# Fixed orders in the dense part and the routing, and expert weights in runs of 32 KB into five places

## The chip, the cores and the metric

The kernel runs on one core of one Trainium2 chip, in one launch. The metric is device time in microseconds (us), the median of several executions. Five engines work side by side: TensorE (matrix products; PE in the profile, its weight loads PEld), VectorE (DVE), ScalarE (ACT), GpSimd (POOL) and SyncE (SP), which here issues nearly all transfers between the chip's memory (HBM) and the on-chip memory (SBUF). Matrix products land in PSUM, a small memory of accumulators.

## The reference

Two transformer layers over 256 tokens of width 1024, in float32; all weights are read once.

```python
# first layer
n = rmsnorm(x, norm_mix_pre); proj = n @ w_in        # pool part, q/k/v, memory query, gates
merged = g0 * pool(...) @ w_pool_o + g1 * stick_breaking(q, k, v) @ w_sb_o \
       + g2 * cross(xq, rmsnorm(mem, norm_mem) @ w_mem_kv) @ w_x_o
h = x + rmsnorm(merged @ w_out, norm_mix_post)
n2 = rmsnorm(h, norm_ffn_pre); gu = n2 @ w_ffn_in
h = h + rmsnorm((silu(gu[:, :2816]) * gu[:, 2816:]) @ w_ffn_out, norm_ffn_post)
# second layer
h = rms_norm(x, g_mix); parts = h @ w_in_2           # two attentions, an index, two gates
x = x + (sig(ga) * (o_a @ w_proj_a) + sig(gb) * (o_b @ w_proj_b)) @ w_out_2
# 32 experts, each token goes to the best 2 of the 8 in its best group
for each token's two experts e:
    x += gate * ((silu(xt @ w1[e]) * (xt @ w3[e])) @ w2[e])      # 1024 -> 512 -> 1024
out = rms_norm(x, g_final)
```

The experts' weights are 32 x 3 x 1024 x 512 floats, 201 MB; all other weights are 107 MB.

## The kernel before

**Dense part.** Each float32 product is made of three products of split values: an operand is split into a high part (ScalarE copies it to a shorter format, line 179) and a low part (VectorE, seldom GpSimd, subtracts, line 180), and `mm3` multiplies high by high, high by low and low by high (lines 226 to 228). Weights come in chunks of 1 MB (8 KB in each of 128 partitions) into `ring`, four buffers; a chunk is split into two or more "pieces", whose low parts stand in `lows` or `swing`. A chunk's buffer is free when it has been split, and the next load waits for that on SyncE.

The 256 tokens are two tiles (`tt` 0 and 1). `ts_pair` makes 512 columns of a projection for both tiles, piece by piece; `t_unit` makes a transposed block of 256 columns; `rows_mm` makes an output projection over 1024 columns into four accumulators, at its end with `tt_major=True`: all remaining products of tile 0 first, then those of tile 1. Behind it stand `post_norm_add` (norm of the sums, added to `x`) and `normed_T` (norm of `x`, eight transposes `xtp` on TensorE, split into `xhi` and `xlo`), for tile 0 and then tile 1. This happens twice: at about 223 us (before the first feed-forward products `gu`) and at about 413 us (before the projection `qiT`). At the start the first projection `pps` is written out by hand, operation by operation, with an order for each engine (`do`, `hi_split`, `lo_split`, `products`, `transposes`, `evicted`). The memory's norm, with its transposes, is written after the query product `xq`, before the products `mk` and `mvps` that need it.

The order in which each engine takes its instructions is set by a planner that simulates the program with costs of its own. `tc.issue_after(i)` ties an instruction behind `i` on its engine; `tc.high_priority()` moves a stretch ahead. `behind` ties each TensorE step of the routing to the one before.

**Routing.** The last output projection, the router's logits, the choice of experts (`route`), the numbering of tokens within an expert (`rank`), and the gathering of an expert group's 4 x 32 token slots (`slots`, products `gat` with a 0/1 matrix `pm`, evicted to `xs`). Gate values (`gs`, `den`, `gt`) are worked out with no fixed place among these.

**Experts.** Eight groups of four experts. For a group, W1 and W3 have eight chunks each (`hb`, lines 1292 to 1294), then W2 has four for the low and four for the high half of the columns (`yb`); a chunk holds 128 rows of all four experts, 1 MB. `slot_mm` (line 1277) makes four products per chunk, one for each expert, on 32 columns of the array; the profile records eight matmuls for them. Two chunks make a pair of 2 MB, one transfer of 16 KB per partition (line 1200). Eleven places of 16 KB per partition take the pairs in turn:

```python
    order = [places[n] for n in "sw mg gs b2 c2 d2 tu o r0 r1 lo".split()]
```

They lie where buffers of the dense part lay, so a place's first load waits until these are done: `sw` swing, `mg` mgp, `gs` the gain rows and scratch, `b2 c2 d2` the second attention's buffers, `tu` the gates and `o` the attention outputs, `r0 r1` the two halves of `ring`, `lo` `lows`. The last two chunks of the first group's W3 go elsewhere (two half loads `whalf` and one `wchunk`). In the last group, W2's high half comes in smaller transfers: two of 1 MB and four of 0.5 MB.

After the last group the output is normed and written (lines 1348 to 1359).

Of the kernel before, what the change touches and what calls it, by code (L numbers as in the profile page):

```python
# [18 lines left out]
P = 128  # L19
# [62 lines left out]
def block_kernel(ctx: ExitStack, tc: tile.TileContext, A, out: bass.AP):  # L82
# [151 lines left out]
    def t_block(dst, pc, c0, k, act):  # L234
        for kt in range(k):
            mm3(dst, (pc[0][:, kt, c0:c0 + P], pc[1][:, kt, c0:c0 + P]),
                (act[0][:, kt, :], act[1][:, kt, :]), kt == 0, kt == k - 1)
# [21 lines left out]
    def ts_mm(dst, pcs, act, tt):  # L259
        for k0, per, pc in pcs:  # L260
            for j in range(per):
                mm3(dst, cut(act, k0 + j, tt), (pc[0][:, j, :], pc[1][:, j, :]), k0 + j == 0, k0 + j == KT - 1)
# [11 lines left out]
    def ts_pair(src, c0, n, act, name, hold=1, after=(), free=0, aside=()):  # L274
# [3 lines left out]
        group, npc, made = [], KT // per, 0  # L278
        for c in range(KT // kk):
            w = ts_load(src, c0, n, c)  # L280
            for h in range(2):
# [15 lines left out]
    def rows_mm(accs, pcs, get, nk, tt_major=False):  # L297
        if tt_major:
            r = None
            for tt in range(NT):  # L300
                with ExitStack() as q:
                    if r is not None:
                        q.enter_context(tc.issue_after(r.ins))
                    for h in range(2):
                        for kt, pc in pcs:
                            act, kk = get(kt)
                            r = mm3(accs[tt][h], cut(act, kk, tt), (pc[0][:, h, :], pc[1][:, h, :]), kt == 0,
                                    kt == nk - 1)
            return
# [32 lines left out]
    def normed_T(src, g, tt, hi, lo):  # L342
# [3 lines left out]
        for hf in range(2):  # L346
# [7 lines left out]
            for j in range(4):  # L354
                kt = hf * 4 + j
                nc.tensor.transpose(b[:, j * P:(j + 1) * P], n[:, kt * P:(kt + 1) * P], ident)
# [128 lines left out]
    lo_split(3, "G")  # L485
# [4 lines left out]
    evicted(0, 1, True)  # L490
    for i in (2, 3):
        products(0, i, LH)
# [61 lines left out]
    mt = mg_tiles()  # L554
    for tt in range(NT):
        normed_T(mem[tt], g_mem, tt, *mt)
# [118 lines left out]
    def project(src, accs):  # L675
# [3 lines left out]
        rows_mm(accs, rows_pieces(src, 2) + rows_pieces(src, 4) + rows_pieces(src, 6), get, KT, tt_major=True)  # L679
# [6 lines left out]
    project("w_out", accs)  # L686
# [69 lines left out]
    rows_mm(accs, rows_pieces(wfo, 2 * nf - 6) + rows_pieces(wfo, 2 * nf - 4) + rows_pieces(wfo, 2 * nf - 2),  # L756
# [17 lines left out]
    for tt in range(NT):  # L774
        post_norm_add(accs[tt], g_post, EPS, tt)
        first.append(normed_T(x[:, tt, :], g_pre, tt, *xt))
    cneg = at.tile([P, 384], F32, name="cneg")
# [16 lines left out]
    def rope_heads(c0, scale, name, pool, *how):  # L794
        o = ts_pair(w2in, c0, 512, xt, name, *how)
# [122 lines left out]
    for name, c0, pool in (("b", 1536, atb), ("a", 0, at)):  # L918
        qT = rope_heads(c0, 0.125, "qT" + name, pool)
        kT = rope_heads(c0 + 512, 1.0, "kT" + name, pool)  # L920
        o = ts_pair(w2in, c0 + 1024, 512, xt, "v" + name)
# [181 lines left out]
    pms, gats, xss = {}, {}, {}  # L1103

    def slots(g, tt, hf):
# [5 lines left out]
        if hf == 0:  # L1111
            nc.vector.tensor_tensor(out=pm, in0=rk[:, tt, es, None].to_broadcast([P, 4, CAP]),
                                    in1=cst("iota")[:, None, :].to_broadcast([P, 4, CAP]), op=ALU.is_equal)
# [8 lines left out]
        if hf == 0:  # L1122
            xss[g] = dn.tile([P, KT, P], F32, name="xs", tag="whi", bufs=3)
        ks = slice(hf * 4, hf * 4 + 4)
        nc.vector.tensor_tensor(out=xss[g][:, ks, :], in0=b.rearrange("p (k t) -> p k t", k=4),  # L1125
                                in1=gk[:, ks, None].to_broadcast([P, 4, P]), op=ALU.mult)
        return last

    with tc.high_priority():
# [36 lines left out]


    ew = A["experts"].rearrange("(g c) p n -> g c p n", g=8)
    W1, W3, W2 = 0, KT, 2 * KT

    wst.close()
    places = {}
    for side, names in (("left", "r0 r1 lo mg sw gs tu o"), ("right", "b2 c2 d2")):
        for n in names.split():
            places[n] = ctx.enter_context(tc.tile_pool(name="pair" + n, bufs=1, side=side, reuse_waits="tile"))
    order = [places[n] for n in "sw mg gs b2 c2 d2 tu o r0 r1 lo".split()]
    turn_of = {"i": 0}
    pairs = {}

    def pair_tile():  # L1180
        p = order[turn_of["i"] % len(order)]
        turn_of["i"] += 1
        return p.tile([P, 4096], F32, name="wpair", tag="w")

    def single(g, c, t, e0, ne):
        v = t[:, :ne * 512]
        nc.sync.dma_start(out=v, in_=ew[g, c // 2, :, c % 2 * 2048 + e0 * 512:c % 2 * 2048 + (e0 + ne) * 512])
        return [v[:, e * 512:(e + 1) * 512].rearrange("p (h n) -> p h n", h=1) for e in range(ne)]

    def eload(g, c, part=None):  # L1190

        if g == 0 and c == W3 + KT - 1:
            return single(g, c, xp.tile([P, 2048], F32, name="wchunk", tag="xlo"), 0, 4)
        if g == 0 and c == W3 + KT - 2:
            return [r for e0 in (0, 2) for r in single(g, c, dn.tile([P, 1024], F32, name="whalf", tag="whi", bufs=3),
                                                       e0, 2)]
        if part is None:
            if c % 2 == 0:
                pairs["t"] = pair_tile()
                nc.sync.dma_start(out=pairs["t"], in_=ew[g, c // 2])  # L1200
            t = pairs["t"]
            if c >= W2 + 4:
                v = t.rearrange("p (h f e n) -> p h f e n", h=2, f=2, e=4)
                return [v[:, :, c % 2, e, :] for e in range(4)]
            v = t.rearrange("p (f e n) -> p f e n", f=2, e=4)
            return [v[:, c % 2, e:e + 1, :] for e in range(4)]

        f = c - W2 - 4
        if f == 0:
            pairs["t"] = pair_tile()  # L1210
        t = pairs["t"].rearrange("p (f n) -> p f n", f=4)
        if part == 1 or f % 2 == 0:
            n = 1024 if part == 1 else 2048
            nc.sync.dma_start(out=t.rearrange("p f n -> p (f n)")[:, f * 1024:f * 1024 + n],
                              in_=ew[g, c // 2, :, part * 2048 + f % 2 * 1024:part * 2048 + f % 2 * 1024 + n])
        return [t[:, f, e * 256:(e + 1) * 256].rearrange("p (h n) -> p h n", h=1) for e in range(4)]
# [203 lines left out]
```

## Time and profile before

| | |
|---|---|
| time, median of 3 runs | 1064.04 us (1063.94 to 1064.76) |
| time of the profiled execution | 1063.62 us |
| its span (first to last instruction) | 1061.8 us |
| TensorE busy | 909.4 us (86%) |
| VectorE / ScalarE busy | 451.2 us (42%) / 352.5 us (33%) |
| mean granted TensorE clock | 0.949 |
| read from HBM | 308.20 MB |

The profile is one execution. Each of the three runs is timed without it. A row of the chain of work is a piece of the path that ended last, followed back from the end; a row in brackets such as "[0.90 <-ACT xhi L179]" gives the time the engine stood before it and what ended that. Matmuls overlap, so a row's time can reach into the next.

### The profile page before, as it was taken

How to read it: one execution, taken by the hardware profiler on the slowest of the kernel's cores; microseconds unless marked ns; L12 is line 12 of the kernel's file. 1: busy time of each engine (PE TensorE's matmuls, PEld its weight loads, DVE VectorE, ACT ScalarE, POOL GpSimd, SP SyncE). 2: the span in 40 equal slices, each digit the busy share in tenths (PEclk: the TensorE clock that was granted, in tenths of full speed). 3: DMA queues.
4: the chain of work that ended last, by engine and by line, in shares of the span. 5: the costliest groups of instructions: out<-in, count | busy, mean ns of one | idle time of the engine just before them, and what ended most of it. 6: DMA issues, size and time to landing. Idle time of an engine off the chain costs nothing.

```text
span 1061.8 us, 14621 instructions
## 1 busy us (share of the span) xinstructions
PE 909.4 (86%) x6159; PEld 649.3 (61%) x6159; DVE 451.2 (42%) x765; ACT 352.5 (33%) x550; POOL 48.4 (5%) x42
## 2 busy tenths in 40 slices
PE   8999999999999999999999999767565756666555
PEld 6989899979999996878889973312121211212112
DVE  6656546776545546779765741110101000101102
ACT  6645765455444443444675431000000000000002
POOL 2000022000000000212000000000000000000000
PEclk9999999999999999999999999888998798978988
DMA  9644366556555523744456789999999999999995
GB/s 364 246 150 159 110 251 222 215 225 212 196 196 174 194 97 121 315 159 159 159 206 270 310 326 427 429 426 429 426 429 425 427 428 427 428 427 427 428 428 245
DMA packets 32857, 310.27 MB, mean 292 GB/s; under 512 B 3985, under 2 KB 5137, under 8 KB 8721
## 3 DMA queue, kind: packets, MB, share of 16 engines
q1 hardware_dynamic: 32496, 309.18, 73.1%
q8 instruction: 51, 0.84, 0.3%
q14 instruction: 22, 0.17, 0.0%
q10 hardware_dynamic: 288, 0.08, 0.0%
HBM read 308.20 MB, written 1.05 MB: 291 GB/s over the span
## 4 chain that ended last, share of the span: by engine, by line
PE 59%; DMA 36%; DVE 2%; ACT 1%; issue 1%; POOL 0%; POOLq 0%; SPq 0%; ACTq 0%; DVEq 0%
DMA wpair<-in_experts_dram 36%; PE gu L227 4%; PE gu L228 4%; PE gu L226 4%; PE gate L228 4%; PE gate L227 4%; PE gate L226 4%; PE fo L227 2%; PE fo L226 2%; PE fo L228 2%; PE hb L1277 2%; PE y L228 2%; PE y L226 2%; PE y L227 2%; PE wo L227 1%; PE wo L226 1%
## 5 line engine op out<-in xcount | busy, mean ns | idle before, releaser
L180 DVE TENSOR_TENSOR wlo<-wchunk,whi 128x1024 fp32r<-128x1024 f32 x146 | 181.5, 1250 | 108.1 <-ACT whi L179 106.5
L1277 PE MATMUL hb<-wpair,xs 128*32 128x512 f32 x1008 | 142.6, 695 | 85.9 <-DMA wpair<-in_experts_dram 80.8
L179 ACT ACTIVATE whi<-wchunk 128x1024 fp32r<-128x1024 f32 (+1 forms) x151 | 156.7, 1048 | 164.2 <-PE gu L227 30.2
L1277 PEld LDWEIGHTS hb<-wpair,xs 128*32 128x32 f32 x1008 | 30.2, 119 | 187.1 <-DMA wpair<-in_experts_dram 119.5
L1277 PE MATMUL yb<-wpair,mw 128*32 128x512 f32 (+1 forms) x544 | 74.2, 678 | 32.0 <-DMA wpair<-in_experts_dram 30.5
L1341 DVE TENSOR_TENSOR x<-x,comb 128x512 f32<-128x512 f32 (+1 forms) x34 | 22.3, 656 | 132.7 <-PE comb L1339 132.6
L228 PE MATMUL gate<-xhi,wlo 128*128 128x256 f32 x256 | 73.3, 287 | 0.0
L226 PE MATMUL gate<-xhi,whi 128*128 128x256 f32 x256 | 73.0, 285 | 0.0
L227 PE MATMUL gate<-xlo,whi 128*128 128x256 f32 x256 | 72.7, 284 | 0.0
L1277 PEld LDWEIGHTS yb<-wpair,mw 128*32 128x32 f32 x544 | 16.9, 122 | 82.9 <-DMA wpair<-in_experts_dram 45.5
L1125 DVE TENSOR_TENSOR xs<-gat,gains 128x512 f32<-128x512 f32 x16 | 11.1, 692 | 117.7 <-PE gat L1117 117.7
L180 DVE TENSOR_TENSOR wsw<-wchunk,wsw 128x1024 fp32r<-128x1024 f32 x35 | 42.8, 1224 | 38.3 <-ACT wsw L179 38.1
L226 PE MATMUL gu<-xhi,whi 128*128 128x256 f32 x192 | 54.0, 281 | 0.0
L228 PE MATMUL gu<-xhi,wlo 128*128 128x256 f32 x192 | 54.0, 281 | 0.0
L227 PE MATMUL gu<-xlo,whi 128*128 128x256 f32 x192 | 53.9, 280 | 0.0
L1304 ACT ACTIVATE mw<-hT 128x512 f32<-128x512 f32 x8 | 4.8, 597 | 144.7 <-PE hT L1302 144.7
L179 ACT ACTIVATE wsw<-wchunk 128x1024 fp32r<-128x1024 f32 (+1 forms) x38 | 39.7, 1047 | 33.8 <-PE gu L228 11.0
L228 PEld LDWEIGHTS gate<-xhi,wlo 128*128 128x128 f32 x256 | 48.2, 188 | 2.2 <-issue 2.2
L227 PEld LDWEIGHTS gate<-xlo,whi 128*128 128x128 f32 x256 | 48.2, 188 | 0.8 <-issue 0.5
L226 PEld LDWEIGHTS gate<-xhi,whi 128*128 128x128 f32 x256 | 48.4, 189 | 0.4 <-issue 0.4
L1336 ACT ACTIVATE ysb<-yb 128x512 f32<-128x512 f32 (+1 forms) x17 | 9.7, 572 | 114.9 <-PE yb L1277 114.9
L1296 ACT ACTIVATE ms<-hb 128x512 f32<-128x512 f32 x8 | 4.8, 597 | 128.4 <-PE hb L1277 128.4
(486 smaller groups left out, 1982.2 us busy)
## 6 DMA issues: line engine op xcount, KB each, us to landing
wpair<-in_experts_dram SPq DMA_DIRECT2D x93, 2048.0 KB, 39.1
wchunk<-in_dense_dram SPq DMA_DIRECT2D x92, 1024.0 KB, 4.9
wchunk<-in_dense_dram SPq DMA_DIRECT2D x6, 512.0 KB, 6.1
wpair<-in_experts_dram SPq DMA_DIRECT2D x2, 1024.0 KB, 35.9
wpair<-in_experts_dram SPq DMA_DIRECT2D x4, 512.0 KB, 25.6
memt<-in_mem_dram SPq DMA_DIRECT2D x2, 512.0 KB, 11.9
wchunk<-in_experts_dram SPq DMA_DIRECT2D x1, 1024.0 KB, 10.0
whalf<-in_experts_dram SPq DMA_DIRECT2D x2, 512.0 KB, 8.5
```

What stands on the lines that cost most here:

```text
L179: a = nc.scalar.activation(hi, src, AF.Copy)
L180: return a, (eng or nc.vector).tensor_tensor(out=lo, in0=src, in1=hi.bitcast(F32), op=ALU.subtract)
L226: nc.tensor.matmul(o, lhsT=lh[0], rhs=rh[0], start=start, stop=False)
L227: nc.tensor.matmul(o, lhsT=lh[0], rhs=rh[1], start=False, stop=False)
L228: return nc.tensor.matmul(o, lhsT=lh[1], rhs=rh[0], start=False, stop=stop)
L1125: nc.vector.tensor_tensor(out=xss[g][:, ks, :], in0=b.rearrange("p (k t) -> p k t", k=4), in1=gk[:, ks, None].to_broadcast([P, 4, P]), op= ...
L1277: nc.tensor.matmul(o[ps, :].rearrange("p (h n) -> p h n", h=m), lhsT=lhsT[:, ps], rhs=w[e], start=first, stop=last, skip_group_check=True, ...
L1296: nc.scalar.activation(s, hb[0], AF.Silu)
L1304: nc.scalar.activation(mw[:, 1, :], b, AF.Copy)
L1336: nc.scalar.activation(y[:, cs], yb[:, :n], AF.Copy)
L1341: nc.vector.tensor_tensor(out=xa, in0=xa, in1=cb[:, :n], op=ALU.add)
```

## The change

It has two parts. In the dense part and the routing, orders are tied that were left to the planner:

- the low part of piece 3 in the first projection moves from GpSimd to VectorE, behind tile 0's evictions;
- `xq` is made in two halves, each set behind the transposes of one tile of the memory;
- `rows_mm` with `tt_major` returns `rest`, which issues the last two of tile 1's twelve steps of three products behind the first tile's transposes;
- `ts_pair` gets `in_order`, used by all second-layer projections but `qiT`;
- the routing issues the first two chunks' products `hb` before the last `slots` step; `xs` of the first half is evicted in four pieces; the gate arithmetic stands behind the last `xs`, and `pm` of group 1 too.

The experts' weights are laid out so that four chunks (a quad) are one run of 32 KB per partition, 4 MB in one transfer, into five places of 32 KB, with one of 16 KB (`d`) for two chunks of the first group only. `mgp` and `swing` move ahead of `ring` in memory so that `ms` joins them, `r` is the whole ring, `lu` is `lows` with the gain rows and scratch, `to` the gates and attention outputs, `b` and `d` the second attention's buffers. In the last group W2's high half comes as one transfer of 2 MB and four of 0.5 MB.

```diff
+    mgp = wst.enter_context(tc.tile_pool(name="mgp", bufs=2, side="left"))
+    swing = wst.enter_context(tc.tile_pool(name="swing", bufs=2, side="left"))
     ring = wst.enter_context(tc.tile_pool(name="ring", bufs=4, side="left"))
     lows = wst.enter_context(tc.tile_pool(name="lows", bufs=2, side="left"))
-    mgp = wst.enter_context(tc.tile_pool(name="mgp", bufs=2, side="left"))
-    swing = wst.enter_context(tc.tile_pool(name="swing", bufs=2, side="left"))
...
                     for tt in range(NT):
-                        ts_mm(o[tt][:, :n], group, act, tt)
+                        with ExitStack() as q:
+                            if r is not None and in_order:
+                                q.enter_context(tc.issue_after(r.ins))
+                            r = ts_mm(o[tt][:, :n], group, act, tt)
...
+            todo = [(h, kt, pc) for h in range(2) for kt, pc in pcs]
+            for a in todo:
+                r = one(0, *a)
+            with tc.issue_after(r.ins):
+                for a in todo[:-2]:
+                    one(1, *a)
+
+            def rest(ins):
+                with tc.issue_after(ins.ins):
+                    for a in todo[-2:]:
+                        one(1, *a)
+            return rest
...
     hi_split(3)
-    lo_split(3, "G")
     products(0, 3, HH)
     scaled(1)
     products(0, 2, HL)
     transposes(1)
     evicted(0, 1, True)
+    lo_split(3, "V")
     for i in (2, 3):
         products(0, i, LH)
     products(0, 3, HL)
...
-    b = t_unit(w, xt, "xq")
+    b = t_tile("xq")
+    mt = mg_tiles()
+    r = ()
+    for tt in range(NT):
+        pc = piece(w[:, :, tt * P:(tt + 1) * P], KT, P)
+        normed_T(mem[tt], g_mem, tt, *mt, r)
+        with tc.issue_after(turned_last[tt].ins):
+            r = (t_block(b[:, tt * S:(tt + 1) * S], pc, 0, KT, xt),)
...
     for tt in range(NT):
         post_norm_add(accs[tt], g_post, 4 * EPS, tt)
         first.append(normed_T(x[:, tt, :], g_pre, tt, *xt))
+        if tt == 0:
+            rest(turned_last[0])
...
+    for side, names in (("left", "ms r lu to"), ("right", "b d")):
+        for n in names.split():
+            places[n] = ctx.enter_context(tc.tile_pool(name="place" + n, bufs=1, side=side, reuse_waits="tile"))
+    order = [places[n] for n in "ms b to r lu".split()]
...
+        if part is None:
+            if c % 4 == 0:
+                held["t"] = place_tile()
+                nc.sync.dma_start(out=held["t"], in_=ew[g, c // 4])
...
         route(1)
-        for tt, hf in ((0, 1), (1, 0), (1, 1)):
+        for tt, hf in ((0, 1), (1, 0)):
             behind(lambda: slots(0, tt, hf))
-
-
+        hbs = {0: acc_tile("hb")}
+        for kt in range(2):
+            behind(lambda: slot_mm(hbs[0][0], xss[0][:, kt, :], eload(0, W1 + kt), kt == 0, False))
+        behind(lambda: slots(0, 1, 1))
+
+    gq = ExitStack()
+    gq.enter_context(tc.issue_after(xs_last[0].ins))
```

## Rows read from the trace of the kernel before

**Rows 1.** The page: moved data in 40 slices; the chain's shares.

```profile
GB/s 364 246 150 159 110 251 222 215 225 212 196 196 174 194 97 121 315 159 159 159 206 270 310 326 427 429 426 429 426 429 425 427 428 427 428 427 427 428 428 245
...
PE 59%; DMA 36%; DVE 2%; ACT 1%; issue 1%; POOL 0%; POOLq 0%; SPq 0%; ACTq 0%; DVEq 0%
```

**Rows 2.** Windows, TensorE: us of the window, busy (records), clock, DMA share, GB/s.

```profile
474.00:600.00 126.00, 126.00 (x929) 1.00 0.55 202
```

**Rows 3.** Timeline of SP's issues, 597 to 634 us: start, us, line, transfer.

```profile
597.57 0.33 SPq L1200 DMA_DIRECT2D wpair<-in_experts_dram  x1
...
600.76 0.33 SPq L1200 DMA_DIRECT2D wpair<-in_experts_dram  x1
...
602.74 0.33 SPq L1200 DMA_DIRECT2D wpair<-in_experts_dram  x1
...
613.74 0.33 SPq L1200 DMA_DIRECT2D wpair<-in_experts_dram  x1
...
620.32 0.33 SPq L1200 DMA_DIRECT2D wpair<-in_experts_dram  x1
...
633.16 0.33 SPq L1200 DMA_DIRECT2D wpair<-in_experts_dram  x1
```

**Rows 4.** Windows, transfers: us, clock, DMA share, GB/s.

```profile
610.00:640.00 30.00, 1.00 0.88 338
640.00:1036.00 396.00, 0.88 1.01 427
1038.00:1041.00 3.00, 1.00 1.00 419
1043.00:1046.00 3.00, 0.67 1.02 412
```

**Rows 5.** Chain of work in order of time, 610 to 720 us.

```profile
631.24 13.87 PE hb L1277 x128
...
677.00 39.09 DMA wpair<-in_experts_dram
```

**Rows 6.** Instructions of the tile `wpair`: its transfers from issue to landing.

```profile
DMA to landing us min/median/max: 7.9/39.1/40.8
```

**Rows 7.** Timeline of the start, VectorE, GpSimd and TensorE.

```profile
6.54 0.88 DVE L435 TENSOR_SCALAR ntok<-x,rsr 128x512 f32<-128x512 f32 x2 [0.67 <-POOL rsr L430]
...
13.61 2.98 DVE L435 TENSOR_SCALAR ntok<-x,rsr 128x512 f32<-128x512 f32 x2
...
13.46 2.44 POOL L409 TENSOR_TENSOR wlo<-wchunk,whi 128x1024 fp32r<-128x1024 f32 x1 [0.49 <-ACT whi L406]
...
16.25 1.11 PE L442 MATMUL xtp<-ck,ntok 128*128 128x128 f32 x8 [1.62 <-DVE ntok L435]
```

**Rows 8.** Timeline of TensorE at the memory's norm.

```profile
70.19 0.39 PE L226 MATMUL mvps<-wsw,mgh 128*128 128x256 f32 x1 [1.12 <-ACT mgh L179]
```

**Rows 9.** Timeline of TensorE at the first feed-forward norm.

```profile
224.51 0.50 PE L226 MATMUL gu<-wsw,xhi 128*128 128x512 f32 x1 [0.45 <-ACT xhi L179]
```

**Rows 10.** Timeline of TensorE at the second layer's norm.

```profile
415.23 0.47 PE L226 MATMUL qiT<-wsw,xhi 128*128 128x512 f32 x1 [0.90 <-ACT xhi L179]
...
422.63 1.29 PE L356 MATMUL xtp<-ck,ntok 128*128 128x128 f32 x8 [0.67 <-DVE ntok L349]
```

**Rows 11.** Chain of work at the second layer's norm, 413 to 425 us.

```profile
412.99 0.23 PE fo L227
...
417.52 1.22 DVE wlo L180
...
419.34 1.80 DVE wlo L180 x2
```

**Rows 12.** Timeline of TensorE at the third projection of the second layer.

```profile
472.97 0.50 PE L226 MATMUL qTa<-whi,xhi 128*128 128x512 f32 x1 [0.74 <-DVE vb L924]
```

**Rows 13.** Timeline of TensorE at the end.

```profile
1041.20 4.48 PE L1277 MATMUL yb<-wpair,mw 128*32 128x512 f32 x32 [2.60 <-DMA wpair<-in_experts_dram]
...
1050.16 1.67 PE L1277 MATMUL yb<-wpair,mw 128*32 128x256 f32 x24
```

More of the change, by code (lines that the diff above doesn't have):

```diff
@@ L272, in ts_load, with ts_pair @@
         return t.rearrange("p (k n) -> p k n", k=kk)
-    def ts_pair(src, c0, n, act, name, hold=1, after=(), free=0, aside=()):
+    def ts_pair(src, c0, n, act, name, hold=1, after=(), free=0, aside=(), in_order=False):
         o = acc_tile(name)
@@ L277, in ts_pair @@
         per = kk // 2
-        group, npc, made = [], KT // per, 0
+        group, npc, made, r = [], KT // per, 0, None
         for c in range(KT // kk):
@@ L298, in rows_mm, with one @@
         if tt_major:
[L299 to L309, printed above, removed]
+            def one(tt, h, kt, pc):
+                act, kk = get(kt)
+                return mm3(accs[tt][h], cut(act, kk, tt), (pc[0][:, h, :], pc[1][:, h, :]), kt == 0, kt == nk - 1)
+            todo = [(h, kt, pc) for h in range(2) for kt, pc in pcs]
[9 more added lines that the diff above has]
+            return rest
         for kt, pc in pcs:
@@ L794, in rope_heads @@
     def rope_heads(c0, scale, name, pool, *how):
-        o = ts_pair(w2in, c0, 512, xt, name, *how)
+        o = ts_pair(w2in, c0, 512, xt, name, *how, in_order=not how)
         if how:
@@ new lines, in block_kernel, with place_tile, by_chunk, single @@
+    turn_of = {"i": 0}
+    held = {}
+    def place_tile():
+        p = order[turn_of["i"] % len(order)]
+        turn_of["i"] += 1
+        return p.tile([P, 8192], F32, name="wquad", tag="w")
+    def by_chunk(t, m):
+        v = t.rearrange("p (f e n) -> p f e n", f=m, e=4)
+        return [[v[:, f, e:e + 1, :] for e in range(4)] for f in range(m)]
+    def single(g, c, t, e0, ne):
+        v = t[:, :ne * 512]
+        o0 = c % 4 * 2048 + e0 * 512
+        nc.sync.dma_start(out=v, in_=ew[g, c // 4, :, o0:o0 + ne * 512])
+        return [v[:, e * 512:(e + 1) * 512].rearrange("p (h n) -> p h n", h=1) for e in range(ne)]
@@ new lines, in eload @@
+    def eload(g, c, part=None):
+        if g == 0 and c == W3 + KT - 1:
+            return single(g, c, xp.tile([P, 2048], F32, name="wchunk", tag="xlo"), 0, 4)
+        if g == 0 and c == W3 + KT - 2:
+            return [r for e0 in (0, 2) for r in single(g, c, dn.tile([P, 1024], F32, name="whalf", tag="whi", bufs=3),
+                                                       e0, 2)]
+        if g == 0 and c // 2 == (W3 + KT - 4) // 2:
+            if c % 2 == 0:
+                t = places["d"].tile([P, 4096], F32, name="wtwo", tag="w")
+                nc.sync.dma_start(out=t, in_=ew[g, c // 4, :, :4096])
+                held["c"] = by_chunk(t, 2)
+            return held["c"][c % 2]
+        if part is None:
+            if c % 4 == 0:
+                held["t"] = place_tile()
+                nc.sync.dma_start(out=held["t"], in_=ew[g, c // 4])
+            t = held["t"]
+            if c >= W2 + 4:
+                v = t.rearrange("p (h f e n) -> p h f e n", h=2, f=4, e=4)
+                return [v[:, :, c % 4, e, :] for e in range(4)]
+            return by_chunk(t, 4)[c % 4]
+        f = c - W2 - 4
+        if part == 0 and f == 0:
+            held["t"] = place_tile()
+        o0, n = part * 4096 + f * 1024, 1024 if part == 1 else 4096
+        if part == 1 or f == 0:
+            nc.sync.dma_start(out=held["t"][:, o0:o0 + n], in_=ew[g, c // 4, :, o0:o0 + n])
+        v = held["t"][:, o0:o0 + 1024]
+        return [v[:, e * 256:(e + 1) * 256].rearrange("p (h n) -> p h n", h=1) for e in range(4)]
@@ L1105, in slots, with slot_mm @@
+    def slot_mm(o, lhsT, w, first, last):
+        for e in range(4):
+            ps = slice(e * 32, e * 32 + 32)
+            m = w[e].shape[1]
+            r = nc.tensor.matmul(o[ps, :].rearrange("p (h n) -> p h n", h=m), lhsT=lhsT[:, ps], rhs=w[e], start=first,
+                             stop=last, skip_group_check=True, tile_position=(0, e * 32))
+        return r
+    pms, gats, xss, xs_last = {}, {}, {}, {}
     def slots(g, tt, hf):
@@ L1165, in block_kernel @@
     nc.vector.tensor_copy(cnt, cmx)
[L1168 to L1216, printed above, removed]
+    gq.close()
     def overflow():
@@ L1271, in overflow @@
                                                            in1=xa, op0=ALU.mult, op1=ALU.add)
-    def slot_mm(o, lhsT, w, first, last):
-        for e in range(4):
-            ps = slice(e * 32, e * 32 + 32)
-            m = w[e].shape[1]
-            nc.tensor.matmul(o[ps, :].rearrange("p (h n) -> p h n", h=m), lhsT=lhsT[:, ps], rhs=w[e], start=first,
-                             stop=last, skip_group_check=True, tile_position=(0, e * 32))
     WHOLE = ((0, 512), (512, 512))
```

74 lines of the change are left out of this document (44 added, 30 removed).

## The prediction

> **What bounds the kernel now.** I read the page first. Its chain of work [rows 1] has two long links: TensorE with 59% of the span and one DMA stream, the expert weights, with 36%. Its GB/s row shows where one hands over to the other: about 200 GB/s for the first 20 slices, then 427 for the last 16. So there are two stages with different limits, and I read each by itself.
>
> The dense stage, to about 600 us, is TensorE's. The window from 474 to 600 us shows it busy in all of 126.00 us [rows 2], at full clock, and the others up to there look the same but for the gaps named below. There only a gap can be won, and what is won arrives whole at the end of the stage, since all later work follows on it.
>
> The expert stage is the DMA's: 427 GB/s from 640 to 1036 us [rows 4], and eight 2 MB pairs take 39.1 us, 4.89 each [rows 5]. 201 MB (96 pairs) must come. How late the end is depends on four things: when the stream can run without a break, how many pairs are left then, how long one takes, and what TensorE does after the last one. In the 30 us from 610 to 640 the stream moved 338 GB/s [rows 4], so (427 − 338)/427 × 30 = 6.3 us of stream time were lost there: pairs were issued at 613.74 and 620.32, as places came free, and the next, the first into a place used once already, only at 633.16 [rows 3], when TensorE had read the first pair (it starts on the experts at 631.24 [rows 5]).
>
> **The change, part by part.** *Places.* Before, each of the eleven places takes one pair; the last two of these first loads are those at 613.74 and 620.32 [rows 3], so nine were issued ahead of them. After, `to` needs both the gates and the attention outputs free (600.76), `r` the whole ring, so the half that was free at 602.74 waits for 613.74, and `lu` for 620.32. By 613.74 places `ms`, `b`, `to` and `d` have been issued, seven pairs, not nine. Two pairs more must come after that: +2 × 4.89 = +9.8 us. On the other side the stream then has no break: 4 + 4 + 2 MB (`r`, `lu` and the three single loads) are 24.5 us of work issued from 613.74, enough to about 639, and the first place to be reused, `ms`, comes free when TensorE has read four chunks. 128 matmul records in 13.87 us [rows 5] make 3.5 us for the 32 of a quad, so it is free near 635, also with the 16 `gat` products (some 1 us) that now stand between its second and third chunk. Of the 6.3 us lost, the part between the landing of the load before and the first bytes of the one issued at 613.74 stays; the three pairs issued from 597.57 on need 14.7 us, so they were in about when the next was issued, and a pair's shortest landing, 7.9 us [rows 6], holds 3.0 us beside the 4.89 of moving, for its start and its finish. I put the start at 1.4 us. 4.9 us go. **Net +4.9 us.** The routing edits (first two chunks ahead of the last `gat`, gate arithmetic behind `xs`) lie in front of TensorE's expert work, with the stream busy over it; I cost them at nothing. Their cover is the 4 us between 635 and 639; without it they would cost what passes that.
>
> *Runs of 32 KB.* The trace has no such run. It has three sizes: 427 GB/s at 16 KB, 419 at 8 KB and 412 at 4 KB [rows 4], that is 4.91 us for 2 MB, 2.50 for 1 MB and 1.27 for 0.5 MB. Two transfers in place of one cost 0.095 us more at the first halving (2 × 2.50 − 4.91) and 0.043 at the second. I take 0.085 for the next doubling, near the closer row, a little less because the windows of 3 us are coarse. From `r` on 43 whole quads come: **−3.7 us**, bounds 43 × 0 and 43 × 0.095 = −4.1; that a larger run is slower I leave out, as both steps go one way.
>
> The Trainium skill (DMA: Bandwidth & Descriptors, "Why small descriptors are slow (HBM only)") says that a packet carries a fixed overhead of about 3 cycles on a path of 32 B beats and that joining packets pays only at small sizes. An estimate from that page: 3 in 515 cycles at 16 KB and 3 in 1027 at 32 KB are 0.3% of 9.79 us, 0.03 us per quad, −1.2 us in all, and the sum below would be −1.9 + 2.5 = +0.6 us.
>
> *The end.* The last whole quad of the last group lands when its second pair did before, and TensorE then has 32 matmul records to do, not 16. From 1041.20 on it works almost without a break into its last products from 1050.16 on [rows 13], so the extra 16 count: 1.7 us at the rate of [rows 5], twice that at half the clock (the 32 at 1041.20, half of them of half width, took 4.48 us where that rate makes 2.6), less what it gives back at the wait for the last landing. I take **+1.0 us**, bounds 0 and +3.
>
> *Start.* The two `ntok` scalings of token tile 1 take 2.98 us while GpSimd makes a low part (13.46, 2.44 us), where the same pair took 0.88 for tile 0; TensorE waits 1.62 us for them [rows 7]. With that low part on VectorE behind the four evictions (1.22 us, as one of the same size in [rows 11]), the scalings end near 14.6 and TensorE's transposes (1.11 us) and four products (0.9) follow at once, to 16.5; the evictions (1.1) and the split make the low part ready at 16.9, and the products with it wait 0.4 us. −1.6 + 0.4: **−1.2 us**, bounds 0 and −1.6.
>
> *Memory norm.* TensorE stands 1.12 us between the memory's transposes and the first product with them [rows 8]. With the two `xq` halves set between the transposes, each half (24 products of 256 columns, about 2.8 us) covers an eviction: **−1.1 us**; nothing excludes that the filler runs out, bound 0.
>
> *Postponed last products.* `rest` holds back six products of 512 columns (0.23 us each [rows 11], 1.4 us) of tile 1 until tile 0's transposes are issued, so that they cover its eviction. At the first norm the gap is 0.45 us [rows 9]; but tile 1's sums end one set of transposes later (1.0 us), and its own norm starts late by as much. There tile 0's 48 `gu` products (11 us) cover that: −0.5 us, bounds −0.7 (a short wait for the low half goes too) and +0.5. At the second norm the gap is 0.90 us, and 0.67 follow where TensorE waits for tile 1's `ntok` [rows 10]. That chain has VectorE's `wlo` splits within it, 1.22 and 1.80 us [rows 11], which could now run in the stretch in which VectorE waits for the later sums. If they do, the chain shortens by up to 3 us less the 1.0; if not, it is 1.0 longer. I take −1.0 us, bounds −2.5 and +1.0. **Together −1.5 us.**
>
> *`in_order`.* The products of a piece for tile 0 stand ahead of those for tile 1. It removes no work; the one gap of these projections is 0.74 us, at the copy of `vb` [rows 12]. **−0.3 us**, bounds −0.7 and +0.5.
>
> Sum: +4.9 − 3.7 + 1.0 − 1.2 − 1.1 − 1.5 − 0.3 = −1.9 us. The profiled execution took 1063.6 us (span 1061.8), 0.4 below the median 1064.0 of the three: 1061.7 for such an execution, **1062.1** against the median.
>
> **The rivals.**
> *Larger runs gain little.* If a doubling saves only what the smaller step of [rows 4] shows, 43 × 0.043 = 1.8 us, or nothing, the time is 1062.1 + 1.9 = 1064.0 to 1062.1 + 3.7 = 1065.8. For it: both steps are under a fiftieth already. Against: the nearer one is the larger. The overhead that the page of the Trainium skill gives would come out within this, at 1064.6.
> *The ties win more.* If the second norm's chain loses all its splits (−2.5 in place of −1.0) and the first norm, the projections and the start reach their bounds (−0.2, −0.4, −0.4 more), and the end costs nothing, −1.9 − 1.5 − 1.0 − 1.0 gives 1058.6. For it: all the splits do stand in that chain. Against: VectorE has to do them before TensorE's products anyway.
> *Slower: `r` is issued behind `lu`.* SP works in order. If the transfer for `r` stands behind the one for `lu`, it goes at 620.32, not 613.74 [rows 3], and the stream stands 6.6 us longer: 1068.7. It decides from 4.0 us of delay on, when the time is over 1066.2. Against: the two were issued in the order of their places now; for it: both are written after the single loads and move ahead by the planner's choice alone.
> *The ties do nothing*, if the planner had this order already: the dense terms (−4.1) fall away, 1066.2. The start speaks against that, as the engine of a split changes there.
>
> **How the numbers follow.** A measurement of this kernel tells 0.2%, 2.1 us, from no change. The forecast has 0.55, with a range of its own from 1058.9 to 1065.0 (dense terms ±2.5, end and runs ±1.5 beside them), about half of it below 1061.9. Little gain by the runs has 0.17, more by the ties 0.13, `r` late 0.10, no ties 0.05. Faster: 0.55 × 0.5 + 0.13 = 0.41. Slower (over 1066.2): 0.10 + 0.05 = 0.15. The same: the rest, 0.44. The range for 8 in 10 goes from 1058.3, a little under the larger gain of the ties, to 1066.5, past the case without ties.
>
> **What would show it.** Right: 7 pairs' worth landed and 4 MB issued near 609.6 (613.74 less the dense 4.1); no break in the GB/s between that issue and the end; about 9.70 us between landings of quads (9.79 if runs gain nothing); TensorE's transposes of tile 1 in the first projection near 14.7 and not 16.25, no gap near 69, 223 or 413, and tile 1's `ntok` at the second norm no later than now. Wrong: `lu` ahead of `r`, a break before the first reuse, or TensorE still in the last `yb` over 1.5 us after the last landing.

## The result, and the profile after

The changed kernel takes 1070.58 us, the median of five runs (1067.78 to 1071.09), against 1064.04 (1063.94 to 1064.76): the ratio is 1.0052, with a 95% interval from 1.0041 to 1.0064. It is 0.5% slower, where 0.2% faster was forecast, and it lies beyond the upper end of the range, 1066.5. The profiled execution took 1071.07 us, its span is 1069.2; before they were 1063.62 and 1061.8.

The page of the changed kernel, the rows that answer to [rows 1]: GB/s in 40 slices, and the chain's shares.

```profile
GB/s 359 246 168 140 134 231 248 208 126 231 173 187 213 149 138 115 276 158 158 158 126 280 301 409 439 431 429 431 429 432 432 426 432 432 432 430 430 431 431 209
...
PE 63%; DMA 33%; DVE 2%; ACT 1%; issue 1%; SPq 0%; POOLq 0%; POOL 0%; DVEq 0%; ACTq 0%
```

The stream is where the gain was meant to be, and it came: 431 GB/s where 427 stood. TensorE's share of the chain grew from 59% to 63%, but that alone does not say where the time went: by the two pages the experts' own products `hb` and `yb` make 7% of the chain now, where `hb` made 2% and `yb` did not stand in the list. The timelines below say it. The windows of transfers, to be read beside [rows 4] (us, clock, DMA share, GB/s), show less lost from 610 to 640, and a long window that is a little faster.

```profile
610.00:640.00 30.00, 1.00 0.97 409
640.00:1036.00 396.00, 0.86 1.00 431
```

SP's issues in the changed kernel, the timeline that answers to [rows 3]; they are `to`, `r`, `lu` and the first place to be used again:

```profile
606.79 0.33 SPq L1172 DMA_DIRECT2D wquad<-in_experts_dram  x1
...
617.22 0.33 SPq L1172 DMA_DIRECT2D wquad<-in_experts_dram  x1
...
623.79 0.33 SPq L1172 DMA_DIRECT2D wquad<-in_experts_dram  x1
...
639.93 0.33 SPq L1172 DMA_DIRECT2D wquad<-in_experts_dram  x1
```

The order is the forecast one, `r` ahead of `lu`. The hour is not: `r` goes at 617.22 where 609.6 was forecast, and where its last half went at 613.74 before. The dense part, meant to be 4.1 us shorter, is 3.5 us longer. TensorE's timeline in the changed kernel shows where, read against [rows 7], [rows 9], [rows 10] and [rows 12]:

```profile
16.01 1.03 PE L458 MATMUL xtp<-ck,ntok 128*128 128x128 f32 x8
...
222.96 0.40 PE L226 MATMUL gu<-wsw,xhi 128*128 128x512 f32 x1
...
228.74 0.50 PE L226 MATMUL gu<-whi,xhi 128*128 128x512 f32 x1 [1.03 <-ACT whi L179]
...
231.08 0.50 PE L227 MATMUL gu<-wlo,xhi 128*128 128x512 f32 x1 [0.43 <-DVE wlo L180]
...
418.18 0.76 PE L226 MATMUL qiT<-wsw,xhi 128*128 128x512 f32 x1 [4.17 <-DVE pn L383]
...
476.40 0.50 PE L226 MATMUL qTa<-whi,xhi 128*128 128x512 f32 x1 [0.75 <-DVE vb L949]
```

The gap ahead of the second tile's transposes at the start is gone. At the first norm the 0.45 us ahead of `gu` are gone too, but 1.03 and 0.43 us stand a little later. At the second norm TensorE waits 4.17 us for the first `qiT` product, where it waited 0.90. The first `qTa` product, my mark for the dense part from here on, comes at 476.40; before it was at 472.97 [rows 12]: 3.43 us late.

The other two engines at the second norm of the changed kernel. VectorE:

```profile
410.97 0.69 DVE L383 TENSOR_TENSOR pn<-fo,grow 128x512 f32<-128x512 f32 x1
412.85 1.29 DVE L180 TENSOR_TENSOR xlo<-xtp,xhi 128x512 fp32r<-128x512 f32 x2 [1.19 <-ACT xhi L179]
414.28 3.03 DVE L180 TENSOR_TENSOR wlo<-wchunk,whi 128x1024 fp32r<-128x1024 f32 x3
417.23 0.20 DVE L348 TENSOR_SCALAR rsm<-ss 128x1 f32<-128x1 f32 x1
417.36 0.68 DVE L383 TENSOR_TENSOR pn<-fo,grow 128x512 f32<-128x512 f32 x1
```

ScalarE:

```profile
413.19 2.58 ACT L179 ACTIVATE whi<-wchunk 128x1024 fp32r<-128x1024 f32 x3
415.66 0.59 ACT L338 ACTIVATE sqscr<-fo 128x512 f32<-128x512 f32 x1
```

And the windows of TensorE there (us, busy, clock, DMA share, GB/s):

```profile
410.00:414.00 4.00, 4.00 (x22) 1.00 0.00 0
414.00:418.00 4.00, 0.01 (x1) 0.80 0.17 45
418.00:422.00 4.00, 3.82 (x9) 0.50 0.94 377
422.00:424.00 2.00, 2.00 (x7) 0.69 0.64 270
424.00:430.00 6.00, 5.75 (x29) 1.00 0.01 3
```

Tile 1's last sum ends at 414.01. Its square on ScalarE and its reading into `pn` on VectorE then stand in their queues behind three pieces of weights, and the `pn` that TensorE waits for ends at 418.04. When the products start again the granted clock is 0.50, the level of 1.2 GHz, and it stays there into the window from 422.

In the kernel before, that `pn` on VectorE and tile 0's `xhi` on ScalarE came at nearly the same time, ahead of the weights:

```profile
414.41 0.68 DVE L367 TENSOR_TENSOR pn<-fo,grow 128x512 f32<-128x512 f32 x1
414.14 1.08 ACT L179 ACTIVATE xhi<-xtp 128x512 fp32r<-128x512 f32 x2
```

and the window there (busy time of TensorE, its weight loads, VectorE, ScalarE and GpSimd, then the clock) is at full clock:

```profile
414.00:418.00 4.00, 3.10 (x16) 2.27 (x14) 3.72 (x7) 4.00 (x8) 0.55 (x1) 1.00 0.08 26
```

The end in the changed kernel, the timeline that answers to [rows 13]:

```profile
1046.92 7.51 PE L1192 MATMUL yb<-wquad,mw 128*32 128x512 f32 x64 [3.41 <-DMA wquad<-in_experts_dram]
...
1059.10 0.64 PE L1192 MATMUL yb<-wquad,mw 128*32 128x256 f32 x8
```

A window of TensorE there:

```profile
1047.00:1051.00 4.00, 4.00 (x20) 0.50 0.98 401
```

Some 20 of the 64 run at half the clock. The last piece is issued at 1016.95 and lands 39.8 us later, at 1056.75, 12.4 us ahead of the end of the span. Before, it was issued at 1030.98 and landed 20.2 us later, 10.6 ahead of the end. So the last landing is 5.6 us later and what follows it 1.8 longer. From 1046.92 on TensorE works almost without a break and ends its last `yb` at 1059.74, 3.0 us behind the last landing; before, it ended 0.65 us behind it (1050.16 + 1.67 [rows 13], against 1051.18). More than 1.5 us was one of the prediction's signs of being wrong.

These are the lines of the last piece, of the changed kernel and of the one before:

```profile
DMA to landing us min/median/max: 39.8/39.8/39.8
DMA to landing us min/median/max: 20.2/20.2/20.2
```

### The profile page after: what moved, and what is told of

It reads as the page before. It is cut to its first block, busy times and chain, and to the rows that moved or that the text cites. A ratio compares the mean times of both kernels' runs of the same rounds, so it can differ in the third digit from the quotient of the medians.

```text
span 1069.2 us, 14531 instructions
## 1 busy us (share of the span) xinstructions
PE 918.8 (86%) x6159; PEld 659.1 (62%) x6159; DVE 454.2 (42%) x769; ACT 352.4 (33%) x550; POOL 46.1 (4%) x41
## 4 chain that ended last, share of the span: by engine, by line
PE 63%; DMA 33%; DVE 2%; ACT 1%; issue 1%; SPq 0%; POOLq 0%; POOL 0%; DVEq 0%; ACTq 0%
DMA wquad<-in_experts_dram 32%; PE hb L1192 4%; PE gu L227 4%; PE gu L228 4%; PE gate L228 4%; PE gu L226 4%; PE gate L227 4%; PE gate L226 4%; PE yb L1192 3%; PE fo L226 2%; PE fo L227 2%; PE fo L228 2%; PE y L228 2%; PE y L226 2%; PE y L227 2%; PE wo L226 1%
## 5 line engine op out<-in xcount | busy, mean ns | idle before, releaser
L1192 PE MATMUL hb<-wquad,xs 128*32 128x512 f32 x992 | 148.2, 749 | 81.6 <-DMA wquad<-in_experts_dram 76.3
L179 ACT ACTIVATE whi<-wchunk 128x1024 fp32r<-128x1024 f32 x151 | 156.6, 1047 | 159.7 <-PE gu L227 31.9
L1192 PEld LDWEIGHTS hb<-wquad,xs 128*32 128x32 f32 x992 | 36.1, 132 | 186.6 <-issue 99.3
L1192 PE MATMUL yb<-wquad,mw 128*32 128x512 f32 (+1 forms) x544 | 74.8, 702 | 33.8 <-DMA wquad<-in_experts_dram 33.4
L1224 DVE TENSOR_TENSOR xs<-gat,gains 128x512 f32<-128x512 f32 (+1 forms) x19 | 11.3, 606 | 171.0 <-PE gat L1213 161.0
L1192 PEld LDWEIGHTS yb<-wquad,mw 128*32 128x32 f32 x544 | 20.0, 130 | 82.3 <-issue 70.0
```

Of the source, the lines that this page charges most:

```text
L179: a = nc.scalar.activation(hi, src, AF.Copy)
L1192: r = nc.tensor.matmul(o[ps, :].rearrange("p (h n) -> p h n", h=m), lhsT=lhsT[:, ps], rhs=w[e], start=first, stop=last, skip_group_check=T ...
L1224: xs_last[g] = nc.vector.tensor_tensor(out=xss[g][:, ks, :], in0=b[:, j * P:(j + m) * P].rearrange("p (k t) -> p k t", k=m), in1=gk[:, ks, ...
```

## The experiments

Twelve kernels, in three sets of four; the kernel before ran beside each set, with medians of 1064.58, 1064.63 and 1064.47 us. The theory at the outset: the postponed products cost the dense part some 4 us, the coarse places and the end the rest.

### The second norm, and the two halves of the change

**norm2_whole**: at the second norm tile 1's products follow tile 0's at once. (It is six products that `rest` holds back; where the expectations say four, they mean these.)

```diff
+    rest(None)
     for tt in range(NT):
         post_norm_add(accs[tt], g_post, EPS, tt)
         first.append(normed_T(x[:, tt, :], g_pre, tt, *xt))
-        if tt == 0:
-            rest(turned_last[0])
```

> The changed kernel, but at the second norm the four last products of tile 1 follow tile 0's at once, as before the change. Theory (the postponed products cost the dense part 3.8 us at the second norm, because the bank that the first product of the 64-column keys needs is read out behind three low-part subtractions): that product starts within 1 us of the last output product, the dense part ends some 3.5 us earlier, the stream's last block lands 3.5 us earlier, and the time is 1066.6 to 1067.6. Rival (the five coarse places set the stream's end whatever the dense part does): the last block lands within 1 us of the changed kernel's and the time stays at 1069.5 to 1070.6.

Measured: 1066.38 us, 1.0013 (1.0004 to 1.0022) of before. `qTa` starts at 472.33, 4.07 us earlier than in the changed kernel. That one tie held two thirds of the loss by the medians, and three quarters by the ratios to the kernel before.

**norm2_freed_ahead**: the tie stays, but the weight pieces are ordered behind the reading of tile 1's sums.

```diff
-        post_norm_add(accs[tt], g_post, EPS, tt)
+        freed = post_norm_add(accs[tt], g_post, EPS, tt)
...
-    qiT = rope_heads(3072, 1.0, "qiT", at, 4, first[0], 2)
+    qiT = rope_heads(3072, 1.0, "qiT", at, 4, (freed,), 2)
...
-    pc = piece(w, KT, 72)
+    pc = piece(w, KT, 72, (freed,))
```

> The changed kernel with the postponed products kept, but with the low parts of the three weight pieces at the second norm ordered behind the reading out of tile 1's bank. Theory (it is the place in VectorE's queue that costs, not the postponement): the gap ahead of the keys' first product falls from 4.2 to about 1.5 us, and the time to 1067.5 to 1068.5. Rival (the postponement itself costs): the gap and the time stay within 0.8 us of the changed kernel's, 1069.8 to 1070.8.

Measured: 1066.57 us, 1.0021 (1.0012 to 1.003). Its chain of work, and TensorE's timeline:

```profile
414.86 0.60 DVE pn L383
415.46 2.94 DVE wlo L180 x3
```

```profile
415.61 0.47 PE L226 MATMUL qiT<-wsw,xhi 128*128 128x512 f32 x1 [1.77 <-DVE pn L383]
```

With `pn` ahead of the three `wlo`, `qiT` starts 0.15 us behind it, and `qTa` is at 472.56. So it is the place in the queues that cost (on ScalarE the square of tile 1's sums is no longer held up either, 413.93 against 415.66, so this run does not tell the two queues apart); the postponement itself costs next to nothing, and brings nothing. After 1.77 us of idle time the clock was still at 1.00, so both parts of the loss went, and the time is 1 us under what I expected.

**places_alone**: five places, 32 KB runs and the routing, with all ties of the dense part undone. **ties_alone**: the reverse, the ties on the old eleven places and the old routing.

> The kernel before with the five places, the 32 KB runs and the new order in the routing, without any of the ties in the dense part. Theory (the places add 4.9 us of transfers after the release of the first places, the larger runs give back 3.7 and the end loses 1.8): 1066 to 1068, with the dense part within 0.5 us of the kernel before. Rival 1 (the dense part is the whole loss): 1063.5 to 1065. Rival 2 (the places are the whole loss): 1069.5 to 1071.

> The kernel before with the ties of the dense part only: the eleven places of 16 KB and the old routing stay. Theory (dense part 3.5 us later, the same stream and end): 1067 to 1068. Rival 1 (the ties gain, the places lose): 1061.5 to 1063. Rival 2 (no effect, the stream hides it): 1063.5 to 1064.5.

Measured: places_alone 1067.89 us, 1.0028 (1.0017 to 1.0039); ties_alone 1067.10 us, 1.0021 (1.0011 to 1.0031). Both theories of a single cause fall: each half loses by itself, and the two make up the whole (1.0028 × 1.0021 = 1.0049, measured 1.0052). In places_alone `qTa` is 0.6 us late (its first weights were 0.7 late) and the last landing 3.1, so places and runs together cost the stream 2.5.

### The clock, the other ties, the end and the runs

**gap_kept_warm**: 36 products of 256 columns on a constant, used by nothing, behind tile 1's last sum.

```diff
         if tt == 0:
-            rest(turned_last[0])
+            r = rest(turned_last[0])
+            with tc.issue_after(r.ins):
+                heat(36, lambda _, fn: fn())
```

> The changed kernel with 36 small products, whose result nothing uses, put into TensorE's 4.17 us of idle time at the second norm. They take away no wait. Theory (the idle time costs twice: itself, and because the products behind it run at half the clock for 4.8 us, 0.43 us each in place of 0.23, some 2.3 us): the granted clock stays at 1.00 from 418 on, the keys' last product comes 2 us earlier, and the time is 1068 to 1069. Rival (only the wait costs; the slow products are hidden behind VectorE's work for tile 1): the time stays at 1070 to 1071.

Measured: 1068.04 us, 1.0032 (1.002 to 1.0044). Windows of TensorE in it:

```profile
414.00:418.00 4.00, 3.88 (x33) 1.00 0.31 71
418.00:422.00 4.00, 4.00 (x19) 1.00 0.99 414
```

The wait is as long as it was, `qiT` starts at 417.55, but at full clock: 19 product records in the four us from 418 where the changed kernel has 9. From `h0t` (behind the first norm) to the first of the `kiwi` products beside `qiT` this kernel loses 1.45 us against before, the changed one 3.79: 2.3 us were the clock's.

**ties_norms_whole**: the ties on the old places, with whole products at both norms.

> The kernel before with the ties of the memory norm, of the start's last low part and of the two pairs of projections, but with tile 1's products whole at both norms; places and routing as before. Theory (the memory norm gives 1.3 us, the start 0.5 to 1.2, nothing is lost at the norms): 1062.0 to 1063.0, faster than the kernel before. Rival 1 (an earlier dense part is not an earlier end, since the first places come free by other work): 1063.8 to 1064.8. Rival 2 (the other ties lose too): above 1065.

Measured: 1062.59 us, 0.9983 (0.9974 to 0.9992), as the theory had it. The other ties do win, 2.3 us at `qTa` (470.63).

**norms_whole_fine_end**: the changed kernel with whole products at both norms and finer transfers in the last group. **norms_whole_halves**: the same cut in all groups (`if c < W2 + 4 or g == 7`).

```diff
-                nc.sync.dma_start(out=held["t"], in_=ew[g, c // 4])
+                if g == 7:
+                    for o in (0, 4096):
+                        nc.sync.dma_start(out=held["t"][:, o:o + 4096], in_=ew[g, c // 4, :, o:o + 4096])
+                else:
+                    nc.sync.dma_start(out=held["t"], in_=ew[g, c // 4])
```

> The changed kernel with tile 1's products whole at both norms, and in the last of the eight groups each 32 KB run fetched as two of 16 KB, the next to last transfer as two of 8 KB. Theory (the coarse last transfers make the end 1.5 us longer: the products wait for a whole block, then come at half the clock, and are still behind when the last piece lands): the span ends 10.7 to 11.2 us after the last landing and the time is 1064 to 1065. Rival (the end is set by the last DMA engine, 5 to 6 us behind the first, and not by the size of the transfers): 12 us behind the last landing, 1065.5 to 1066.5.

> As the kernel with the fine end, but with every block of 32 KB runs of the first two matrices and the first half of the third fetched as two transfers of 16 KB runs in all eight groups; the five places stay. Theory (a block of 32 KB runs streams 0.085 us faster than two of 16 KB runs; some 36 blocks are cut): 3 us slower than the fine end, 1067 to 1068. Rival (the larger runs gain nothing; what the earlier rows showed is the pairing of the transfers): within 0.7 us of the fine end.

Measured: fine end 1064.14 us, 0.9993 (0.9985 to 1.0002); halves 1066.56 us, 1.002 (1.0011 to 1.0028). In the fine end the last landing is at 1033.15 + 19.8 = 1052.95, 9.8 us ahead of the end of the span (10.7 to 11.2 were expected): the end gave back more than it had lost. This kernel changes two things at once, and only its trace tells them apart: no run has whole products at both norms with the coarse end. Halves cuts 34 more blocks and is 2.4 us slower, 0.07 us a block; at the ends of the two intervals it would be 0.03 or 0.13. The windows of the stream from 660 to 1020, first of the fine end:

```profile
660.00:1020.00 360.00, 0.85 1.00 430
```

and of the halves:

```profile
660.00:1020.00 360.00, 0.82 1.01 428
```

### The terms one by one, and a better version

**first_turn_halves**: the fine end, but in its first turn each 16 KB part is a place of its own, and the parts are joined when that turn is over.

```diff
+    open_places("right", "b d", ctx)
+    open_places("left", "m s r0 r1 lo gs tu o", turn1)
...
+        if not order:
+            turn1.close()
+            open_places("left", "ms r lu to", ctx)
```

> The kernel with the fine end and whole products at both norms, but the first blocks come into places of 16 KB, each as soon as its part of the old buffers is free, and only after that are the places joined to 32 KB. Theory (merging places kept some 6 us of transfers back until after 617, of which the larger runs gave half back): the first turn's last transfer lands some 6 us earlier, the second turn starts with the first release near 636 instead of 639, and the time is 1060 to 1062, below all kernels so far. Rival (the time of the first release was the bound all along, and the merged places cost nothing): 1063.5 to 1064.5.

Measured: 1060.60 us (1059.5 to 1062.38), 0.9966 (0.9953 to 0.9979). It beats both kernels, and the fine end by 3.5 us. SP's issues in it, `tu`, `r0`, `lo`, and the first block of the second turn:

```profile
600.88 0.33 SPq L1181 DMA_DIRECT2D wtwo<-in_experts_dram  x1
...
611.36 0.33 SPq L1181 DMA_DIRECT2D wtwo<-in_experts_dram  x1
...
617.93 0.33 SPq L1176 DMA_DIRECT2D wtwo<-in_experts_dram  x1
...
634.07 0.33 SPq L1191 DMA_DIRECT2D wquad<-in_experts_dram  x1
```

In the fine end the stream is still busy with the first turn when the first place comes free (issue at 634.58, the first turn landed at 641.7); here the first turn has landed at 634.9 and the second starts with that release. The yield is as expected; the kernel also makes the first group's outputs in the finer steps of the last one, and no run tells that from the places.

**norms_alone**, **memory_norm_alone**, **start_alone**: one tie each, on the kernel before.

> The kernel before with one edit alone: the four last products of tile 1 wait for tile 0's transposes at both norms. Theory (0.6 us lost at the first norm, 3 to 4 at the second, of which some 2 by the clock after 4.2 us of idle time): the dense part ends 3.5 to 4.4 us later and the time is 1067 to 1068.5. Rival (the prediction's: 1.5 us gained): 1062.6 to 1063.6.

> The kernel before with one edit alone: the memory's norm goes between the two halves of the cross query's products. Theory (1.3 us gained ahead of the attention, all of it kept): all later products 1.3 us earlier and the time 1063.0 to 1063.6. Rival (the first release or the stream hides it): 1064.2 to 1065.

> The kernel before with one edit alone: the fourth low part at the start is made by VectorE, behind the second tile's scaling and turning, and not by GpSimd. Theory (the 1.6 us gap ahead of the second tile's transposes goes, but the low part is then late: 0.5 us gained): the last projection product of the start comes 0.4 to 0.7 us earlier against the first one, time 1063.8 to 1064.5. Rival (the prediction's 1.2 us): 1.0 to 1.4 us earlier, 1063.0 to 1063.8.

Measured: norms_alone 1069.15 us, 1.0043 (1.0028 to 1.0057); memory_norm_alone 1064.20, 0.9998 (0.9989 to 1.0007); start_alone 1063.18, 0.9987 (0.9978 to 0.9995). start_alone went with its rival, the 1.2 us of the prediction, and not with the 0.5 that I had come to expect.

norms_alone repeats the wait and the clock on the kernel before; `qTa` is at 477.67, 4.7 us late. The time went past my expectation by 0.7 us. TensorE's timeline and, below it, its windows:

```profile
419.31 0.77 PE L226 MATMUL qiT<-wsw,xhi 128*128 128x512 f32 x1 [4.17 <-DVE pn L383]
```

```profile
419.00:423.00 4.00, 3.69 (x9) 0.50 0.93 371
```

memory_norm_alone went against the theory: no gain clear of the noise. TensorE's timeline in it:

```profile
17.51 1.11 PE L458 MATMUL xtp<-ck,ntok 128*128 128x128 f32 x8 [1.77 <-DVE ntok L451]
...
472.88 0.50 PE L226 MATMUL qTa<-whi,xhi 128*128 128x512 f32 x1 [0.75 <-DVE vb L947]
```

This execution began 1.26 us late (17.51 against 16.25 in [rows 7]) and is 0.09 early at `qTa`, so the tie did win its 1.3 us of TensorE. The stream lost about half of it again: the last piece lands at 1051.71, 0.56 us later than before, where `qTa` is 0.09 early (in ties_norms_whole `qTa` is 2.34 early and the last landing, at 1049.57, only 1.58). SP's issues in memory_norm_alone show where:

```profile
600.69 0.33 SPq L1223 DMA_DIRECT2D wpair<-in_experts_dram  x1
...
613.68 0.33 SPq L1223 DMA_DIRECT2D wpair<-in_experts_dram  x1
```

The issue that stood at 602.74 [rows 3] is gone; two pairs go at 613.68 and behind it. Windows of transfers, in this kernel:

```profile
610.00:615.00 5.00, 1.00 0.18 33
```

and in the kernel before:

```profile
610.00:615.00 5.00, 1.00 0.99 370
```

The addresses in the two built programs say why: of the last four weight blocks of the dense part, the last two lay in one half of the ring before (`r1`), so that `r0` came free early; here they lie in different halves, the very last in `r0`, which is read to the end, and the issue for `r1` stands behind that for `r0`. ties_norms_whole has the same order. In the changed kernel it costs nothing, as `r` waits for both halves in any case.

## Why the prediction was wrong

**The step that failed: "Postponed last products", −1.5 us.** It measured +0.6 at the first norm (TensorE is 0.94 us ahead of before on the last `wo` product that is not held back, 220.47 against 221.41, and 0.32 on `h0t`) and +3.8 at the second (from 0.32 us ahead to 3.47 behind on the first `kiwi` product): +4.4, off by 5.9 of the 8.5 us between forecast and median. norms_alone gives +4.7 us of time for it by itself. The prediction's own sign failed as well: tile 1's transposes at the second norm, behind its `ntok`, are at 426.13 and not at 422.63 [rows 10]. Three things in the step were wrong.
- I took the 0.90 us of [rows 10] at its word: released by tile 0's `xhi`. Behind that stood a second condition that had been met 0.13 us earlier, the reading of tile 1's sums into `pn` (`pn` from 414.41 to 415.09 before, `xhi` to 415.22). The trace names the last releaser only. norm2_freed_ahead shows it: `qiT` moves with `pn`. The built programs show why: `qiT` takes two neighbouring accumulators, in which the first half of tile 0's sums and the second half of tile 1's stood; its first product waits until both have been read.
- I saw that the weight pieces could run while VectorE waits for the later sums, and counted it as a gain of up to 3 us. They did run there. Being in the queue first, they were then ahead of the `pn` that TensorE waited for: 3.03 us on VectorE, 2.58 on ScalarE.
- I had no term for the clock. After 4.17 us of idle time some 12 products of 512 columns ran 0.43 us apart and not 0.23. The Trainium skill (TensorE: Matmul & The Clock Gate, "Wait — 56ns, not 53.3ns?") gives 426.7 ns for 512 columns at 1.2 GHz; the trace agrees. gap_kept_warm took 2.5 us off the time by the clock alone (2.1 by the ratios, whose intervals just overlap; the trace's 2.3 us stand beside it). At the first norm no idle time was longer than 1.03 us.

**What the dense part lost as a whole.** Of the 3.43 us at `qTa`, 1.73 arose ahead of everything that the change ties: in the profiled execution of the changed kernel ScalarE began on the first piece of weights at 8.30 us, before at 6.57. In the twelve other kernels that start scatters from 6.77 to 8.11, so it is not shown to be the change's. Counted from that piece, `qTa` is 1.70 us later, not 3.43: +4.4 for the two norms, and −2.7 for start and memory norm. The other runs add up the same way: start_alone −1.4, memory_norm_alone −1.4, ties_norms_whole −2.7, norms_alone +4.5.

**Places, +4.9 us: right in kind, some 1 us short.** Order, unbroken stream and the late `r` came as written. Places and runs together cost the stream 2.5 us (places_alone) where 1.2 was forecast; with the runs at −3.0 to −3.6 the places are 5.5 to 6.1. first_turn_halves gives 3.5 us of it back.

**Runs of 32 KB, −3.7 us: right.** 431 against 427 GB/s is 0.9% of some 390 us, 3.6 us, and quads land 9.72 us apart, where two pairs took 9.80. The cut of 34 blocks costs 0.07 us a block, 3.0 for 43, against the 0.085 taken from [rows 4]. The estimate from the Trainium skill (DMA: Bandwidth & Descriptors, "Why small descriptors are slow (HBM only)") was 0.03; here the rows of sizes nearby were the better guide.

**The end, +1.0 us: +1.8, within its bounds.** The 64 product records from 1046.92 on end at 1054.43, some 20 of them at half the clock, and push the rest back, so that TensorE is still in `yb` 3.0 us behind the last landing. The fine end removes it: there the last `yb` ends 0.7 us behind (1053.64, against 1052.95).

**Start, −1.2 us: right in size.** The transposes were forecast near 14.7; in ties_norms_whole they start at 14.61. In start_alone `qTa` is 1.4 us earlier, counted from the first piece of weights, and the time 1.3 us shorter. In the profiled execution of the changed kernel they start at 16.01 only because the first weights came 1.73 us later: in both kernels they start 7.7 us behind ScalarE's first piece (8.30 here, 6.91 there).

**Memory norm, −1.1 us: −1.3 of TensorE's time.** That an edit there could move the ring's last blocks and with them a place of the stream was not in the prediction; in the changed kernel it does not count.

**`in_order`, −0.3 us: nothing seen.** The gap is 0.75 us, and was 0.74 [rows 12]. No run has this tie by itself; ties_norms_whole, which has it, gains at `qTa` what start and memory norm give without it.

Of the rivals, none told this. `r` was not behind `lu`, and the ties did not do nothing: they did harm, a case that I had bounded at +1.5 us for both norms together. Without that term the same sum gives 1063.6, 0.4 us under the kernel before. norm2_whole, which keeps the tie at the first norm (+0.6), measured 1.8 us over the kernel before that ran beside it; of the 1.6 us that remain, places and runs (+1.3) and the end (+0.8) give somewhat more than all. Added up, the terms as measured make +6.1 us for the changed kernel, where the medians lie 6.5 apart; each comes from single executions, so the agreement to half a microsecond is in part luck.

## What to carry to other kernels

Before tying work behind a wait, list all conditions of the instruction that waits, not only the releaser that the trace names, and look at what the queues of the other engines will do first in the time that falls free; the work that frees the accumulators must stay ahead of work that is only early. A gap of some microseconds on TensorE is to be priced with the products behind it at half the clock. Larger transfers pay in a steady stream, but where buffers come free bit by bit, and at the end, they want small places and small pieces: both can be had, by joining the places after the first turn.

## What the runs showed of the hardware that I had not expected

- At the second norm the clock fell to 0.50 after 4.17 us without products and came back only 4.8 us after they had started again (418.18 to about 423); in ties_alone, with the same gap, after some 3 us. With 1.77 us of idle time there (norm2_freed_ahead) or 0.90 (before) it stayed at 1.00.
- The parts of one transfer do not land together: the first and the last of the last piece's sixteen landings lie 4.2 to 6.2 us apart, in executions of nearly the same stream, and the piece counts as landed only with the last.
- The first piece of weights was ready for ScalarE at 6.57 to 8.30 us in the profiled executions of these kernels, a scatter of 1.7 us ahead of everything else. The runs of one of the twelve kernels lie 1.4 to 5.1 us apart.
